# Two middle column blocks of an embedding gate joined into one, with three of eight pairs of k tiles in seven products

## The chip, the cores and the metric

The kernel runs on one core of a Trainium2 chip. The metric is device time in microseconds of one execution; a smaller number is better. PE is TensorE (the matmul engine), DVE is VectorE, ACT is ScalarE, SP is the engine that issues most DMAs. All matrices are float32. To get float32 accuracy from the fast matmul format, each operand is split into a high part (`hi`, a cast on ACT) and a low part (`lo`, the difference, a subtraction on DVE), and each product of two 128-row tiles takes three matmuls: low times high, high times high, high times low.

## The reference, cut to what matters

The layer is a decoder layer for 256 tokens of width 2048: a half feed-forward network (FFN), two token mixers, a second half FFN, each followed by a layer norm, and at the end a gated embedding:

```
ple = sigmoid(h @ w_ple_gate) * (p @ w_ple_proj)
h = layer_norm(alpha * h + ple, ln_g[3], ln_b[3])
```

`h` is 256 x 2048 (the result of the norm behind the second FFN), `w_ple_gate` is 2048 x 2048. The change touches only `h @ w_ple_gate`, a product with 16 k tiles of 128, two token halves of 128 and four column blocks of 512.

## The kernel before, in words

**Weights.** A weight chunk is two k tiles by 512 columns, 512 KB. `Chunk` loads it by one SP DMA into a 128x1024 tile (L105); `split` makes it into hi (ACT, L91) and lo (DVE, L92). All such tiles come from one pool of 46 (`SLOTS`).

**The planner.** `plan` is a list of units in the order of use. `Single` is one chunk: 1 tile loaded, 2 made, 12 units of "time". `Seven` is two chunks of the same pair of k tiles in neighbouring column blocks: 2 tiles loaded, 7 kept, time 21. `done(u)` after each unit frees its tiles and calls `fill`, which makes the next loaded unit as long as the time of the ready ones is under `ahead` (45 in this stage) and loads more while ready and loaded are under `far` (90), if the tiles allowed by `slots_for_weights` (24 here) suffice. Every engine runs its instructions in the order in which the Python code issues them, so `fill` also sets the order on DVE and ACT.

**Seven products.** `block` (L321) walks a list of units over a block of 1024 columns. For kind "P" it takes two chunks and adds for each its two k tiles for both token halves: 8 products. For kind "S" it treats two k tiles, two token halves and two column blocks as a 2x2 by 2x2 product and takes 7 products (a Strassen form). That needs four sums of weight tiles (`Seven.make`, L163 to L166, then splits), four sums of activation tiles (`seven_forms`, L362 to L366, then a split), four more PSUM banks, and a fold at the end of the last "S" unit (`seven_common`, L372 to L376). Both FFNs use it, for most blocks in the order "PPSPSPSP" or "PPSSPSSP".

**Side work.** `later(n, job)` puts a job into the list `side`; `run_side`, called after each chunk or unit, takes the first out and issues it.

**The embedding stage.** `embedding` (L1249) takes the four column blocks of the gate one after the other.
- Block 0 begins within the norm behind the second FFN (`norm.first`): six chunks for the first token half, then for the second, while DVE, PE and ACT norm, transpose and split the second half of `ht`, the activations. Then two chunks more.
- Blocks 1 and 2 take eight chunks each (`tokens_chunk`: 2 k tiles by 2 token halves by 3 matmuls = 12 matmuls a chunk).
- Each block has an epilogue per token half, `finish`: a sigmoid from PSUM (ACT, L1254), times the embedding projection, scaled sum with the residual and norm statistics (DVE, L1255 to L1257). The first half's epilogue is issued at the block's end, the second half's goes to `later(1)`, so it comes after the second chunk of the next block.
- Block 3 goes through `held_out` (L399): all eight chunks for the first token half, 6 matmuls each, then `first_done`, which issues that half's last epilogue and final layer norm (L478, L479), and then the eight chunks for the second half. Then the last epilogue, the second half's norm and the output follow with PE idle.

Of the kernel before, what the change touches and what calls it, by code (L numbers as in the profile page):

```python
# [8 lines left out]
F32 = mybir.dt.float32  # L9
F32R = mybir.dt.float32r  # L10
I32 = mybir.dt.int32
AF = mybir.ActivationFunctionType
ALU = mybir.AluOpType
PSUM = bass.MemoryType.PSUM

P = 128
S = 256
# [8 lines left out]
KD = D // P  # L26
# [10 lines left out]
SEVEN = (0, 1, 2, 3)  # L37
# [11 lines left out]
def layer(ctx: ExitStack, tc: tile.TileContext, io):  # L49
    nc = tc.nc  # L50
    sync, act, dve, pool, pe = nc.sync, nc.scalar, nc.vector, nc.gpsimd, nc.tensor
# [8 lines left out]
    def bank(name):  # L60
        return psum.tile([P, 512], F32, tag="ps", name=name)

    def banks(name):
        return [bank(name + str(j)) for j in range(2)]

    def slot(shape, dt, name):
        return slots.tile(shape, dt, tag="slot", name=name)
# [22 lines left out]
    def split(dst_hi, dst_lo, src, lo_engine=None):  # L90
        act.copy(dst_hi, src)  # L91
        (lo_engine or dve).tensor_tensor(dst_lo, src, dst_hi, ALU.subtract)  # L92
# [113 lines left out]
    def take(key):  # L206
        if not ready:
            fill(True)
        u = ready.pop(0)
        assert u.key == key, (u.key, key)  # L210
        return u

    def done(u):
        room["used"] -= u.keeps
        fill()
# [11 lines left out]
    def run_side(n=1):  # L227
        for _ in range(n):
            if side:
                side.pop(0)()  # L230
        if lazy and next(lazy[0], "end") == "end":
            lazy.pop(0)
# [62 lines left out]
    def half_of(a, t):  # L295
        return tuple(x[:, t * P : (t + 1) * P] for x in a)

    def tokens_chunk(chunk, k0, lhs, sums, ts, kks=(0, 1)):
        for t in ts:
            for kk in kks:  # L300
                sums[t].add(half_of(lhs(k0 + kk), t), chunk.columns(kk))
# [11 lines left out]
    def block_units(units, keys):  # L313

        for kind, p in units:
            if kind == "P":
                plan.extend(Single(keys(n, p)) for n in range(2))
            else:
                plan.append(Seven(keys(0, p), keys(1, p)))
# [35 lines left out]
    def seven_forms(full, hi, lo):  # L355


        a11, a21 = (full[:, 0::2, t * P : (t + 1) * P] for t in range(2))
        a12, a22 = (full[:, 1::2, t * P : (t + 1) * P] for t in range(2))
        raw = slot([P, 8, P], F32, "sums")  # L360
        f5, f6, f7, f3 = (raw[:, 2 * j : 2 * j + 2, :] for j in range(4))
        dve.tensor_tensor(f5, a21, a22, ALU.subtract)  # L362
        dve.tensor_tensor(f7, a11, a21, ALU.subtract)
        dve.tensor_tensor(f6, f5, a11, ALU.subtract)
        dve.tensor_tensor(f3, a12, f6, ALU.add)
        split(hi, lo, raw)  # L366
        return lambda e: [(hi[:, 2 * j + e, :], lo[:, 2 * j + e, :]) for j in range(4)]

    def seven_common(p1, p6, p7, q5):

        e, w = slot([P, 2, 512], F32, "eve"), slot([P, 2, 512], F32, "evw")
        act.copy(e[:, 0], p1)  # L372
        dve.tensor_tensor(w[:, 0], e[:, 0], p6, ALU.add)
        dve.tensor_tensor(e[:, 1], w[:, 0], p7, ALU.add)
        dve.tensor_tensor(w[:, 0], q5, w[:, 0], ALU.subtract)
        dve.tensor_tensor(w[:, 1], q5, e[:, 1], ALU.subtract)  # L376
        return e, w
# [6 lines left out]
    def plan_tokens(key, n_k, nk=2):  # L384
        for c in range(n_k // nk):
            plan.append(Single(key + (c,)))
# [69 lines left out]
    def ln_vectors(i):  # L456
        out = []
        for name in ("ln_g", "ln_b"):
            for hf in range(2):
                v = slot([P, 1024], F32, f"{name}{i}_{hf}")  # L460
                sync.dma_start(
                    v, io[name][0, i : i + 1, hf * 1024 : (hf + 1) * 1024].broadcast_to([P, 1024])
                )
                out.append(v)
        return out[:2], out[2:]
# [120 lines left out]
    def load_columns(src, col, name):  # L586
        v = slot([P, 2, 512], F32, f"{name}{col}")
        sync.dma_start(v, src[col])
        return v
# [48 lines left out]
    ht = big.tile([P, KD, 512], F32R, tag="ht", name="xt")  # L638
# [50 lines left out]
    def gu_units(j):  # L689
        if j == 0:  # L690
            return [("P", p) for p in range(KD // 2)]
        order = "PPSSPSSP" if j % 2 == 0 else "PPSPSPSP"
        sevens = list(SEVEN[: order.count("S")])
        plain = [p for p in range(KD // 2) if p not in sevens]
        return [(kind, (sevens if kind == "S" else plain).pop(0)) for kind in order]

    def gu_keys(name, j):
        return lambda n, p: (name + "_gu", j, n, p)
# [217 lines left out]
    def later(n, job):  # L916
        for j in range(n):
            if len(side) <= j:
                side.append(idle)
        side.insert(n, job)  # L920
# [325 lines left out]
        return norm  # L1246


    def embedding(ht, norm, y):  # L1249
        stats = small.tile([P, 2, 4, 6], F32, tag="stats", name="plst", bufs=1)  # L1250

        def finish(blk, ps, sg, t):
            sl = y[blk][:, t]
            act.activation(sg[:, t], ps, AF.Sigmoid)  # L1254
            dve.tensor_tensor(sg[:, t], sg[:, t], pp[blk][:, t], ALU.mult)  # L1255
            dve.scalar_tensor_tensor(sl, sl, ALPHA, sg[:, t], ALU.mult, ALU.add)
            dve.bn_stats(stats[:, t, blk, :], sl)  # L1257

        def last_norm(t, mv, rstd):
            rows = io["out"][0, t * P : (t + 1) * P]  # L1260
            for c in range(4):
                ln_normal(y, t, mv, rstd, g, b, 4 * c, 4)
                at = slice(c * 512, c * 512 + 512)
                (act if t and c % 2 else sync).dma_start(rows[:, at], y[c][:, t])

        lhs = lambda k: (ht[:, k, :S], ht[:, k, S:])
        for blk in range(4):
            pgs = banks(f"pg{blk}")
            sums = [Sum(b, KD) for b in pgs]
            sg = slot([P, 2, 512], F32, f"sg{blk}")  # L1270
            key = ("w_pg", blk)
            if blk == 0:
                for j in range(4):
                    pp[j] = load_columns(pp, j, "ppr")
                steps = [(key + (c,), 2 * c, 0) for c in range(FRONT)]
                norm.first(steps, lhs, [[s] for s in sums], (1, 3, 3, 6, 7, 9, 10))
                slots_for_weights(24)
                for c in range(FRONT, KD // 2):
                    u = take(key + (c,))
                    tokens_chunk(u.chunk, 2 * c, lhs, sums, (0, 1))  # L1280
                    done(u)
            elif blk < 3:
                for c in range(KD // 2):
                    u = take(key + (c,))
                    tokens_chunk(u.chunk, 2 * c, lhs, sums, (0, 1))
                    done(u)
                    run_side()
            if blk < 3:
                finish(blk, pgs[0], sg, 0)
                later(1, lambda blk=blk, pgs=pgs, sg=sg: finish(blk, pgs[1], sg, 1))  # L1290
                if blk == 0:
                    g, b = ln_vectors(3)
                continue

            def first_done():
                finish(3, pgs[0], sg, 0)
                last_norm(0, *ln_stats(stats[:, 0], 3, 0, LN_EPS))

            steps = [(key + (c,), 2 * c, 0) for c in range(KD // 2)]
            held_out(steps, lhs, [[s] for s in sums], lambda t, j: None, first_done, lambda n: None, False)  # L1300
            finish(3, pgs[1], sg, 1)
            last_norm(1, *ln_stats(stats[:, 1], 3, 1, LN_EPS))
# [30 lines left out]
    with tc.manual_schedule():  # L1333
        warm = small.tile([P, 1], F32, tag="nc1", name="warm")
        dve.memset(warm, 0.0)
        act.activation(warm, warm, AF.Silu)
        plan_ffn("f1")
        plan.extend(Single(("w_pp", blk, 0)) for blk in range(2))
        plan_mixers()
        plan.extend(Single(("w_pp", blk, 0)) for blk in range(2, 4))  # L1340
        plan_ffn("f2")
        for blk in range(4):
            plan_tokens(("w_pg", blk), KD)
        kept = sorted({p // 2 for p in SEVEN})
        norm = ffn("f1", 0, ht, None, x_parts, x_columns, (), rows[0])
        norm = mixers(norm.new, norm, rows[0], kept, rows[1])
        norm = ffn("f2", 2, norm.new, norm, norm.keep, rows[1], (), None)
        embedding(norm.new, norm, norm.y)
        assert not (plan or loaded or ready or side or lazy) and not room["used"]
# [100 lines left out]
```

## Time and profile before

| | us |
|---|---|
| median of 3 runs (lowest, highest) | 2313.45 (2310.71, 2315.56) |
| the profiled execution, its own time | 2312.8 |
| its span in the trace | 2311.0 |
| PE busy in the span | 2279.6 (99%) |
| DVE busy | 1871.4 (81%) |
| ACT busy | 1162.9 (50%) |

The span is the time between the first and the last instruction of the trace; the execution's own time is 1.8 us longer. A matmul row of 128x512 lasts 389 ns, but consecutive rows overlap, so that busy time is a count of time covered and not of durations added. Times in the trace are microseconds from the span's start. In a row of the timeline the columns are the start, the duration, the engine, the source line, the operation, and output and inputs with their shapes; a bracket at the end says how long the engine had been idle and what it waited for. A group of rows may be merged into one, with its count at the end.

The stage that is changed lies in the last 5% of the span: block 1 starts at 2231.0, block 2 at 2252.7, block 3 at 2274.4, and the last matmul ends at 2296.3.

### The profile page before, as it was taken

The page shows a single profiled execution, that of the slowest core. Times are in us where ns is not written, and L with a number is a line of the kernel's source. Part 1 is how long each engine was busy: PE and PEld are TensorE (multiplying, and loading weights), DVE is VectorE, ACT ScalarE, POOL GpSimd, SP SyncE. Part 2 cuts the span into 40 slices and gives each one's busy share as a digit, 9 for nine tenths or more (in the row PEclk, how much of TensorE's full clock was granted, in tenths as well). Part 3 has the DMA queues.
Part 4 walks back from the last instruction along what each step waited for, and adds up shares of the span by engine and source line. Part 5 has one row for each costly group of instructions (what it writes and reads, how often), then busy time and mean ns, then how long its engine had stood idle before and what let it go on. Part 6 is the DMA issues. An engine that isn't in the chain of part 4 may idle for free.

```text
span 2311.0 us, 28634 instructions
## 1 busy us (share of the span) xinstructions
PE 2279.6 (99%) x10502; PEld 1887.7 (82%) x10502; DVE 1871.4 (81%) x2348; ACT 1162.9 (50%) x1404; POOL 97.0 (4%) x53
## 2 busy tenths in 40 slices
PE   9999999999999999999999999999999999999997
PEld 7788888888887888888778888888888888888876
DVE  7999999988988874677655555779999999889876
ACT  5555555565553342434554543355565555655432
POOL 0000000000000530133000000000000000000000
PEclk9999999999999999999999999999999999999999
DMA  9566666665587565546556667476666566565771
GB/s 316 164 218 191 194 208 194 197 218 182 201 287 263 176 225 160 170 150 198 159 158 183 184 207 260 161 249 207 192 191 212 182 204 217 172 219 193 289 255 55
DMA packets 193725, 465.70 MB, mean 202 GB/s; under 512 B 14768, under 2 KB 16048, under 8 KB 193584
## 3 DMA queue, kind: packets, MB, share of 16 engines
q1 hardware_dynamic: 191456, 460.91, 60.7%
q10 hardware_dynamic: 2128, 2.97, 0.4%
q8 instruction: 82, 1.34, 0.2%
q14 instruction: 59, 0.48, 0.1%
HBM read 455.43 MB, written 8.39 MB: 201 GB/s over the span
## 4 chain that ended last, share of the span: by engine, by line
PE 95%; DVE 3%; issue 1%; DMA 0%; ACT 0%; DVEq 0%; ACTq 0%
PE f2g L293 3%; PE f2g L291 3%; PE f2g L292 3%; PE f1g L291 3%; PE gt L291 3%; PE f1g L292 3%; PE f1g L293 3%; PE rqk L242 3%; PE gt L292 3%; PE gt L293 3%; PE f2u L291 2%; PE f2u L292 2%; PE f2u L293 2%; PE f1u L292 2%; PE f1u L291 2%; PE f1u L293 2%
## 5 line engine op out<-in xcount | busy, mean ns | idle before, releaser
L92 DVE TENSOR_TENSOR lf_gu<-rf_gu,hf_gu 128x1024 fp32r<-128x1024 f32 (+1 forms) x283 | 334.5, 1215 | 10.1 <-ACT hf_gu L91 9.7
L91 ACT CAST hf_gu<-rf_gu 128x1024 fp32r<-128x1024 f32 (+1 forms) x283 | 282.0, 1046 | 19.1 <-DMA rf_gu<-in_f_gu 18.8
L92 DVE TENSOR_TENSOR lw_in_f<-rw_in_f,hw_in_f 128x1024 fp32r<-128x1024 f32 x148 | 208.2, 1439 | 61.7 <-ACT hw_in_f L91 59.1
L92 DVE TENSOR_TENSOR lf_down<-rf_down,hf_down 128x1024 fp32r<-128x1024 f32 x152 | 180.9, 1221 | 28.2 <-ACT hf_down L91 23.2
L91 ACT CAST hf_down<-rf_down 128x1024 fp32r<-128x1024 f32 x152 | 155.5, 1051 | 77.7 <-DMA rf_down<-in_f_down 24.4
L91 ACT CAST huf_gu<-uf_gu 128x1024 fp32r<-128x1024 f32 x70 | 73.8, 1054 | 158.9 <-DVE uf_gu L164 153.2
L91 ACT CAST hw_in_f<-rw_in_f 128x1024 fp32r<-128x1024 f32 x148 | 145.8, 1051 | 0.2
L291 PE MATMUL f1g<-hf_gu,xt 128*128 128x512 f32 x247 | 97.3, 394 | 5.3 <-ACT hf_gu L91 5.3
L291 PE MATMUL gt<-hw_in_f,ht 128*128 128x512 f32 x256 | 102.5, 400 | 0.0
L292 PE MATMUL gt<-hw_in_f,ht 128*128 128x512 f32 x256 | 99.9, 390 | 0.0
L293 PE MATMUL gt<-lw_in_f,ht 128*128 128x512 f32 x256 | 99.9, 390 | 0.0
L292 PE MATMUL f1g<-hf_gu,xt 128*128 128x512 f32 x247 | 96.9, 392 | 0.0
L293 PE MATMUL f1g<-lf_gu,xt 128*128 128x512 f32 x247 | 96.8, 392 | 0.0
L291 PE MATMUL f2g<-hf_gu,ht 128*128 128x512 f32 x247 | 96.5, 391 | 0.0
L293 PE MATMUL f2g<-lf_gu,ht 128*128 128x512 f32 x247 | 96.2, 389 | 0.0
L292 PE MATMUL f2g<-hf_gu,ht 128*128 128x512 f32 x247 | 96.1, 389 | 0.0
L91 ACT CAST hvf_gu<-vf_gu 128x1024 fp32r<-128x1024 f32 x70 | 73.8, 1055 | 29.7 <-DVE vf_gu L166 29.7
L92 DVE TENSOR_TENSOR luf_gu<-uf_gu,huf_gu 128x1024 fp32r<-128x1024 f32 x70 | 85.3, 1219 | 0.0
L92 DVE TENSOR_TENSOR lvf_gu<-vf_gu,hvf_gu 128x1024 fp32r<-128x1024 f32 x70 | 85.3, 1218 | 0.0
L795 ACT ACTIVATE eve<-eve 128x1024 f32<-128x1024 f32 x20 | 21.2, 1062 | 127.0 <-DVE eve L794 127.0
L291 PE MATMUL f2u<-hf_gu,ht 128*128 128x512 f32 x212 | 83.5, 394 | 0.0
L291 PE MATMUL f1u<-hf_gu,xt 128*128 128x512 f32 x212 | 83.3, 393 | 0.0
(1053 smaller groups left out, 6275.1 us busy)
## 6 DMA issues: line engine op xcount, KB each, us to landing
rf_gu<-in_f_gu SPq DMA_DIRECT2D x351, 512.0 KB, 5.0
rf_down<-in_f_down SPq DMA_DIRECT2D x176, 512.0 KB, 4.5
rw_in_f<-in_w_in_f SPq DMA_DIRECT2D x148, 512.0 KB, 4.1
rw_rv<-in_w_rv SPq DMA_DIRECT2D x32, 512.0 KB, 4.4
rw_ret<-in_w_ret SPq DMA_DIRECT2D x32, 512.0 KB, 4.2
rw_mix<-in_w_mix SPq DMA_DIRECT2D x32, 512.0 KB, 4.5
rw_pg<-in_w_pg SPq DMA_DIRECT2D x32, 512.0 KB, 4.8
rw_att<-in_w_att SPq DMA_DIRECT2D x16, 512.0 KB, 4.1
```

The source lines that it names most:

```text
L91: act.copy(dst_hi, src)
L92: (lo_engine or dve).tensor_tensor(dst_lo, src, dst_hi, ALU.subtract)
L242: pe.matmul(ps[f], hi[:, kk, f * P : (f + 1) * P], rhs(k), start=k == 0, stop=k == n_k - 1,)
L291: pe.matmul(o, al, bh, start=first, stop=False)
L292: pe.matmul(o, ah, bh, start=False, stop=False)
L293: pe.matmul(o, ah, bl, start=False, stop=self.left == 0)
L795: act.activation(g, g, AF.Silu)
```

## The change

Blocks 1 and 2 become one block of 1024 columns, run by `block` with the units `P3 P4 S0 P5 S1 P6 S2 P7` (the number is the pair of k tiles). The plan holds ten single chunks and three seven units for it, where there were sixteen chunks. Ahead of it, `forms_of` makes the activation sums of two groups of four k tiles: `whole` adds the high and low halves of `ht` back to full activations (the FFN had those at hand), then `seven_forms` follows. After the block four adds join the fold's result with the plain sums, and the four epilogues of blocks 1 and 2 go to `later(0)` to `later(3)`, that is, behind the first four chunks of block 3. Block 0 and block 3 keep their code; block 0's second epilogue is run by the joined block's second `run_side`. The order helper `units_of` is taken out of `gu_units` without a change to the FFNs.

```diff
+    def whole(parts, name):
+        full = slot([P, 4, S], F32, name)
+        n = 4 // len(parts)
+        for j, v in enumerate(parts):
+            dve.tensor_tensor(full[:, n * j : n * j + n], v[:, :, :S], v[:, :, S:], ALU.add)
+        return full
+
+    def forms_of(parts, name):
+        hi, lo = (slot([P, 8, P], F32R, name + w) for w in "hl")
+        return seven_forms(whole(parts, name + "w"), hi, lo)
+
+    def units_of(order, sevens):
+        sevens = list(sevens)
+        plain = [p for p in range(KD // 2) if p not in sevens]
+        return [(kind, (sevens if kind == "S" else plain).pop(0)) for kind in order]
+
+    def block_sums(ps, units, n_k):
+        s = sum(kind == "S" for kind, p in units)
+        return [[Sum(ps[t][n], n_k - (2 * s if t and n else s)) for n in range(2)] for t in range(2)]
...
+    PG_UNITS = units_of("PPSPSPSP", (0, 1, 2))
+    pg_keys = lambda n, p: ("w_pg", 1 + n, p)
...
-        for blk in range(4):
+        made = {}
+        for blk in (0, 1, 3):
+            key = ("w_pg", blk)
+            if blk == 1:
+                made.update((g, forms_of([ht[:, 4 * g : 4 * g + 4, :]], f"pgf{g}")) for g in range(2))
+                pgs = [banks(f"pg1{t}") for t in range(2)]
+                got = []
+                block(
+                    "pg", PG_UNITS, pg_keys, lhs, lambda p: made[p // 2](p % 2), block_sums(pgs, PG_UNITS, KD),
+                    lambda *a: got.extend(seven_common(*a)),
+                )
+                for n in range(2):
+                    for t in range(2):
+                        dve.tensor_tensor(got[n][:, t], got[n][:, t], pgs[t][n], ALU.add)
+                for j in range(4):
+                    n, t = j // 2, j % 2
+                    later(j, lambda n=n, t=t: finish(1 + n, got[n][:, t], got[n], t))
+                continue
...
-            elif blk < 3:
-                for c in range(KD // 2):
-                    u = take(key + (c,))
-                    tokens_chunk(u.chunk, 2 * c, lhs, sums, (0, 1))
-                    done(u)
-                    run_side()
-            if blk < 3:
-                finish(blk, pgs[0], sg, 0)
-                later(1, lambda blk=blk, pgs=pgs, sg=sg: finish(blk, pgs[1], sg, 1))
...
+                finish(0, pgs[0], sg, 0)
+                later(1, lambda pgs=pgs, sg=sg: finish(0, pgs[1], sg, 1))
...
-        for blk in range(4):
-            plan_tokens(("w_pg", blk), KD)
+        plan_tokens(("w_pg", 0), KD)
+        block_units(PG_UNITS, pg_keys)
+        plan_tokens(("w_pg", 3), KD)
```

## The prediction, on record before the changed kernel ran

> **What bounds the kernel now.** I read first the page's busy shares and chain, then the stretches of the embedding stage, then VectorE's order of work in it. The chain says that TensorE (PE) sets the time almost everywhere:
>
> ```profile
> PE 95%; DVE 3%; issue 1%; DMA 0%; ACT 0%; DVEq 0%; ACTq 0%
> ```
>
> The stretches show the changed place. The columns are the stretch, its length, then busy time of PE, weight load, VectorE (DVE), ScalarE (ACT), GpSimd, granted clock, DMA share, GB/s. Block 1 runs from 2231.0, block 2 from 2252.7, block 3 from 2274.4 (first token half) and 2285.3 (second); after 2296.3 comes the tail.
>
> ```profile
> 2226.00:2231.00 5.00, 5.00 (x24) 4.14 (x23) 5.00 (x5) 4.97 (x6) 0.00 (x0) 1.00 0.87 272
> 2231.00:2252.70 21.70, 21.70 (x97) 18.00 (x96) 13.96 (x16) 9.33 (x12) 0.00 (x0) 1.00 0.62 221
> 2252.70:2274.40 21.70, 21.70 (x97) 17.96 (x96) 13.07 (x15) 8.60 (x11) 0.00 (x0) 1.00 0.19 56
> 2274.40:2285.30 10.90, 10.90 (x50) 9.03 (x49) 8.15 (x10) 3.80 (x5) 0.00 (x0) 1.00 0.00 1
> 2285.30:2296.30 11.00, 11.00 (x50) 8.86 (x48) 9.49 (x20) 0.60 (x1) 0.00 (x0) 1.00 0.18 70
> ```
>
> PE has no gap from 2231.0 to 2296.3. VectorE is idle 7.7 us in block 1, 8.6 in block 2, 2.8 in block 3's first half: 19.1 us of cover until 2285.3. But in the 5 us before block 1 it has none: it comes out of the norm with its work in arrears, and its timeline shows that it reaches block 0's first epilogue only at 2231.35, when block 1 already runs:
>
> ```profile
> 2224.53 6.90 DVE L92 TENSOR_TENSOR lw_pg<-rw_pg,hw_pg 128x1024 fp32r<-128x1024 f32 x6 [0.26 <-ACT hw_pg L91]
> 2231.35 0.68 DVE L1255 TENSOR_TENSOR sg<-sg,ppr 128x512 f32<-128x512 f32 x1
> 2232.07 0.69 DVE L1256 SCALAR_TENSOR_TENSOR f2y<-f2y,sg 128x512 f32<-128x512 f32 x1
> 2232.79 0.69 DVE L1257 BATCH_NORM_STATS2 plst<-f2y 128x6 f32<-128x512 f32 x1
> ```
>
> **What is removed.** A plain pair of k tiles over two column blocks is 8 products of 3 matmuls, a seven-product pair is 7. Three such pairs save 9 matmuls. A row lasts 389 ns, but rows overlap; start to start is 21.70/96 = 0.226 us. So PE work falls from 192 to 183 matmuls, by **2.04 us** (0.09%). That is all the change can win here.
>
> **What is added, on VectorE.** Prices are start to start, since VectorE rows overlap slightly too. The nearest rows are those of the second half-FFN, which does the same (forms, then a seven unit):
>
> ```profile
> 1528.75 0.42 DVE L362 TENSOR_TENSOR sums<-keep 128x256 f32<-128x256 f32 x1
> ...
> 1531.75 1.23 DVE L92 TENSOR_TENSOR f2fl<-sums,f2fh 128x1024 fp32r<-128x1024 f32 x1 [1.45 <-ACT f2fh L91]
> 1532.89 0.42 DVE L362 TENSOR_TENSOR sums<-keep 128x256 f32<-128x256 f32 x1
> ...
> 1942.41 0.68 DVE L163 TENSOR_TENSOR uf_gu<-rf_gu,rf_gu 128x512 f32<-128x512 f32 x1
> ...
> 1945.14 1.22 DVE L92 TENSOR_TENSOR lf_gu<-rf_gu,hf_gu 128x1024 fp32r<-128x1024 f32 x1
> ...
> 1949.14 1.22 DVE L92 TENSOR_TENSOR f2al<-f2a,f2ah 128x1024 fp32r<-128x1024 f32 x1
> ```
>
> - Forms of one group: 1532.89 − 1528.75 = 4.14 us, the second there 3.82; both hold the wait for ACT's cast (1.45, 1.12), in which VectorE can do nothing else, as its order is fixed. Before each stands a new add of the halves of ht (128x1024, by `whole`). Before has no such add of two fp32r operands. Bounds: 0.61 us (half a 128x1024 row, if it ran at double rate) and 1.44 (the slowest such rows, L92 of w_in_f). I take 1.14, the step of the back-to-back L92 rows (6.90 us for 6), which has the same size and an fp32r operand. Two groups: 4.14 + 3.82 + 2.28 = **10.2 us**.
> - A seven unit's making: 1949.14 − 1942.41 = **6.73** us, against 4 x 1.14 = 4.56 for the four plain chunks it replaces.
> - The fold (L373 to L376) 2.71 us and four adds from PSUM (L794 rows) 2.41.
> - Epilogues (L1255 to L1257): 2.07 us each, as many as before, but the four of blocks 1 and 2 now all fall into block 3's first half instead of one.
>
> The planner's accounts decide the order. At block 1's start four plain chunks are ready (48 units of work, above the 45 it keeps ahead), as now. In VectorE's order: block 0's first epilogue, both forms, the first seven unit (made when the first chunk is done), block 0's second epilogue, two chunks, the second unit, two chunks, and so on. PE uses 24 matmuls (5.44 us) for a pair of plain chunks, 21 (4.76) for a seven unit.
>
> **The sum, step by step.** VectorE: epilogue 2231.35 to 2233.4; forms to 2243.7; first seven unit to 2250.4, its first low part (2.73 us in, 1.22 long) ready at 2247.6. PE: plain pairs 2231.0 to 2241.9, then the first seven unit, whose third matmul needs that low part: **a gap of about 5.3 us** (two matmuls inside it), until 2247.7, and the unit's end at 2252.0 instead of 2246.6. Its successor waits as well: VectorE does the epilogue to 2252.5 and the next chunk to 2253.7. From there VectorE keeps just ahead: units done at 2261.5 and 2270.5, PE's plain last pair ends at about 2279.5 (before: 2274.5). VectorE: two chunks of block 3 to 2275.0, fold to 2277.7, two more chunks to 2280.0, four adds to 2282.4. Then, in turn, one chunk (1.14) and one epilogue (2.07), four times. PE takes a chunk's first half in 6 matmuls, 1.36 us. Chunks 0 to 4 are in time; the low parts of chunks 5, 6, 7 are ready at 2286.8, 2290.0 and 2293.2, and PE waits 0.1, 1.8 and 1.9 us: **3.8 us**. The first half ends at 2294.2, the second (48 matmuls, 10.9) at 2305.1. Beside it VectorE has the last epilogue and the norm of the first token half, 10.0 us as now (2286.2 to 2296.2), so from 2295.2 to 2305.2: just hidden. The tail behind PE's end stays 14.7 us. PE's end was 2296.3, so the shift is 2305.1 − 2296.3 = **+8.8 us**; the 2.04 saved is in it.
>
> **The clock.** One cost more: after gaps PE is slowed. The trace has it before block 1:
>
> ```profile
> 2211.40:2215.00 3.60, 1.66 (x8) 1.08 (x9) 3.53 (x8) 0.74 (x2) 0.00 (x0) 0.99 0.02 5
> 2215.00:2218.40 3.40, 3.40 (x12) 2.72 (x11) 1.28 (x3) 0.59 (x1) 0.00 (x0) 0.50 0.78 230
> ```
>
> PE was busy 46% of 3.6 us, in pieces, and then had half clock for 3.4 us, worth 1.7. The 5.3 us gap will do the same, but the 1.7 lies in PE's slack, since VectorE is what PE waits for until block 3. In block 3 PE is busy 1.36 of each 3.2 us (42%) for two chunks; a half clock there lands on the second half, on the path. Bounds 0 and 1.7; I take 1.0, as the busy share is like the row's and part of the slow stretch would fall into the gaps. The Trainium skill, "TensorE: Matmul & The Clock Gate", section "What's actually happening", says that the clock falls back after an idle window of some 3.4 us. By it block 3, with no gap over 1.9 us, would keep its clock and the sum would stay +8.8; this case's trace speaks for more, since the longest gap before its drop was 2.0 us.
>
> Forecast: 2312.8 (the profiled execution; span 2311.0 and 1.8 around it) + 8.8 + 1.0 = **2322.6 us**. The median of before, 2313.45, is 0.65 higher, inside the spread of its runs (2310.71 to 2315.56), so I leave it.
>
> **Rivals.**
> 1. *TensorE stays the bound* (the other side). If the low parts come in time, only the saved 2.04 remains: 2310.8 us, no measurable change (below 0.2%, 4.6 us, this kernel's measurement can't tell). For it: 19.1 us of idle VectorE before, and an FFN that runs the same pattern of units with PE full. Against: the idle time lies late in each block, the debt at its start. It decides at 2241.9: the first unit's low part must be there, so the 16.3 us from 2231.35 to 2247.6 would have to be 10.6. Chance 0.08.
> 2. *Only the first gap counts.* If block 3's epilogues fit beside its chunks, PE's lateness at 2279.5 remains: +4.8, 2317.6. For it: VectorE would only need some 4 us less in 62. Against: the four epilogues are 8.3 us in a stretch of 10.9 that has to hold five makings too. Chance 0.14.
> 3. *Tiles run out.* Forms (4 tiles), three units (7 each while in use) and block 3's tiles share 46. A raw load or a making that must wait until PE releases a tile closes the circle: PE waits for VectorE, VectorE for PE. In this stage SP already waits for PE before loads, 6.8 us at longest. One such wait on the path: 2322.6 + 6.8 = 2329.4. Against: loads are issued some 90 units, 20 us of PE time, ahead. Chance 0.14.
> 4. *Faster by over 0.2%*: would need more than the saved matmuls give. Chance 0.03. That the product count isn't cut is excluded by the unit list.
>
> **How the numbers follow.** The forecast, 2319 to 2327, gets 0.61. The range takes in rivals 2 and most of 3 and leaves out 1 and 4: 2316 to 2329.5. Slower by over 0.2% (above 2318.1): 0.61 + 0.14 + about half of 0.14 = 0.83; within: 0.08 + the other half = 0.14; faster 0.03.
>
> **What would show it.** In the profile after: 183 PE matmuls in the joined block; a PE gap of about 5 us near 2242 that names VectorE's low part of the first unit; forms from 2233 to 2244 on VectorE; gaps of near 2 us before chunks 6 and 7 of block 3; clock 0.50 behind the first gap, perhaps behind the last. The prediction is wrong if VectorE starts the forms earlier, if the first unit is made before them, or if the 128x1024 add of ht takes far less than 1.14 us.

## The result and the profile after

The changed kernel takes **2322.56 us** (median of 5 runs, 2322.02 to 2325.44) against 2313.45 (5 runs, 2310.71 to 2315.56); the ratio is 1.0043, 95% interval 1.0029 to 1.0058. The forecast was 2322.6 within 2316 to 2329.5. The profiled execution took 2322.76 us with a span of 2321.0, 10.0 us more than before.

The stretches of the embedding stage in the changed kernel (columns as in the prediction: length, busy time of PE, weight load, VectorE, ScalarE, GpSimd, clock, DMA share, GB/s):

```profile
2231.00:2252.00 21.00, 16.23 (x65) 12.67 (x64) 18.43 (x26) 10.37 (x13) 0.00 (x0) 0.88 0.39 119
2252.00:2279.00 27.00, 27.00 (x117) 22.27 (x116) 26.59 (x32) 15.26 (x18) 0.00 (x0) 0.97 0.64 220
2279.00:2295.00 16.00, 13.59 (x59) 10.64 (x58) 15.76 (x21) 5.04 (x7) 0.00 (x0) 1.00 0.00 1
2295.00:2306.00 11.00, 11.00 (x51) 9.04 (x49) 10.44 (x22) 0.60 (x1) 0.00 (x0) 1.00 0.16 61
```

PE, full throughout before, is now busy 16.23 of the first 21.00 us and 13.59 of 16.00 in the third stretch. VectorE, which had 7.7 and 8.6 us to spare in blocks 1 and 2, is busy 26.59 of 27.00. PE's timeline names what it waits for at both places. First the start of the first seven unit:

```profile
2242.93 0.39 PE L293 MATMUL pg<-lw_pg,ht 128*128 128x512 f32 x1
2244.65 0.50 PE L291 MATMUL pgs<-hw_pg,ht 128*128 128x512 f32 x1 [1.33 <-ACT hw_pg L91]
2244.99 0.39 PE L292 MATMUL pgs<-hw_pg,ht 128*128 128x512 f32 x1
2248.82 0.79 PE L293 MATMUL pgs<-lw_pg,ht 128*128 128x512 f32 x1 [3.44 <-DVE lw_pg L92]
```

then the last two chunks of block 3's first token half:

```profile
2289.82 0.39 PE L292 MATMUL pg<-hw_pg,ht 128*128 128x512 f32 x1
2291.09 0.50 PE L293 MATMUL pg<-lw_pg,ht 128*128 128x512 f32 x1 [0.89 <-DVE lw_pg L92]
...
2292.36 0.40 PE L292 MATMUL pg<-hw_pg,ht 128*128 128x512 f32 x1
2294.28 0.50 PE L293 MATMUL pg<-lw_pg,ht 128*128 128x512 f32 x1 [1.52 <-DVE lw_pg L92]
```

Each wait is for a low part, or (the first) for ScalarE's cast of the first unit's weights, queued behind the cast of the activation sums; from 2232 to 2307 PE waits for nothing else. And VectorE's timeline shows why the low part is late: the activation sums stand between block 0's first epilogue and the first seven unit.

```profile
2234.70 1.21 DVE L374 TENSOR_TENSOR pgf0w<-ht 128x1024 f32<-128x1024 f32 x1
...
2238.61 1.23 DVE L92 TENSOR_TENSOR pgf0l<-sums,pgf0h 128x1024 fp32r<-128x1024 f32 x1 [1.11 <-ACT pgf0h L91]
2239.76 1.22 DVE L374 TENSOR_TENSOR pgf1w<-ht 128x1024 f32<-128x1024 f32 x1
...
2243.68 1.23 DVE L92 TENSOR_TENSOR pgf1l<-sums,pgf1h 128x1024 fp32r<-128x1024 f32 x1 [1.11 <-ACT pgf1h L91]
2244.82 0.69 DVE L163 TENSOR_TENSOR uw_pg<-rw_pg,rw_pg 128x512 f32<-128x512 f32 x1
...
2247.55 1.22 DVE L92 TENSOR_TENSOR lw_pg<-rw_pg,hw_pg 128x1024 fp32r<-128x1024 f32 x1
```

The two brackets are all the waits that VectorE has on its way. From block 0's first epilogue (2232.65) to the start of block 3's last low part (2293.01) it is idle for 2.6 of 60.4 us, and 2.2 of them are these two waits for ScalarE's casts of the sums.

Totals of single executions carry a spread from earlier stages. In the eight kernels with the same code up to block 1 (before, changed, a1 to a6), block 0's first epilogue starts on VectorE anywhere from 2229.8 to 2234.6 us (before 2231.35, changed 2232.65). So the experiments are read by two lengths that leave this out. The **stage** runs from that epilogue's first VectorE row to the start of PE's last matmul, the **chain** from it to the first VectorE row of the last epilogue, behind which only the tail follows. Both are read from one profiled execution of each kernel. The ratios are to runs of before made beside that kernel (medians 2313.45 to 2314.44), so they differ a little from quotients of the medians in the table.

| kernel | median us | ratio to before, 95% interval | stage us | chain us |
|---|---|---|---|---|
| before | 2313.45 | | 64.68 | 65.73 |
| changed | 2322.56 | 1.0043 (1.0029 to 1.0058) | 73.34 | 74.39 |
| a1, joined, plain pairs only | 2313.94 | 0.9998 (0.9990 to 1.0007) | 64.68 | 65.73 |
| a2, seven units last | 2322.45 | 1.0038 (1.0025 to 1.0052) | 73.25 | 74.30 |
| a3, a third of the block's matmuls left out | 2320.96 | 1.0032 (1.0020 to 1.0045) | 73.38 | 74.44 |
| a4, two seven units | 2316.33 | 1.0008 (0.9999 to 1.0017) | 66.66 | 67.72 |
| a5, without the adds of ht | 2319.67 | 1.0028 (1.0018 to 1.0037) | 70.83 | 71.89 |
| a6, these adds twice | 2324.76 | 1.0049 (1.0035 to 1.0063) | 75.84 | 76.89 |
| b1, two units, early sums | 2313.13 | 0.9996 (0.9987 to 1.0005) | 63.34 | 64.40 |
| b2, three units, early sums, GpSimd | 2317.22 | 1.0013 (1.0005 to 1.0022) | 63.53 | 64.58 |
| b4, three units, early sums, VectorE | 2316.53 | 1.0010 (1.0001 to 1.0019) | 64.09 | 68.39 |

### The profile page after: what moved, and what is told of

The parts are those of the page before. It is cut to its first block, busy times and chain, and to the rows that moved or that the text cites. A ratio compares the mean times of both kernels' runs of the same rounds, so it can differ in the third digit from the quotient of the medians.

```text
span 2321.0 us, 28679 instructions
## 1 busy us (share of the span) xinstructions
PE 2282.4 (98%) x10493; PEld 1888.6 (81%) x10493; DVE 1897.1 (82%) x2386; ACT 1170.8 (50%) x1413; POOL 97.0 (4%) x53
## 3 DMA queue, kind: packets, MB, share of 16 engines
q8 instruction: 82, 1.34, 0.2%
## 4 chain that ended last, share of the span: by engine, by line
PE 93%; DVE 5%; issue 1%; ACT 0%; DMA 0%; DVEq 0%; ACTq 0%
PE f2g L293 3%; PE f2g L291 3%; PE f2g L292 3%; PE gt L291 3%; PE f1g L291 3%; PE f1g L293 3%; PE f1g L292 3%; PE rqk L242 3%; PE gt L292 3%; PE gt L293 3%; PE f2u L291 2%; PE f2u L292 2%; PE f2u L293 2%; PE f1u L291 2%; PE f1u L292 2%; PE f1u L293 2%
## 5 line engine op out<-in xcount | busy, mean ns | idle before, releaser
L92 DVE TENSOR_TENSOR lf_gu<-rf_gu,hf_gu 128x1024 fp32r<-128x1024 f32 (+1 forms) x283 | 334.4, 1215 | 9.7 <-ACT hf_gu L91 9.1
L92 DVE TENSOR_TENSOR lw_in_f<-rw_in_f,hw_in_f 128x1024 fp32r<-128x1024 f32 x148 | 208.2, 1439 | 61.7 <-ACT hw_in_f L91 59.4
L92 DVE TENSOR_TENSOR lf_down<-rf_down,hf_down 128x1024 fp32r<-128x1024 f32 x152 | 181.0, 1220 | 28.6 <-ACT hf_down L91 22.3
L92 DVE TENSOR_TENSOR luf_gu<-uf_gu,huf_gu 128x1024 fp32r<-128x1024 f32 x70 | 85.3, 1218 | 0.0
L92 DVE TENSOR_TENSOR lvf_gu<-vf_gu,hvf_gu 128x1024 fp32r<-128x1024 f32 x70 | 85.2, 1218 | 0.0
```

## The experiments

The theory: from block 0's first epilogue on, VectorE has no slack left, and its work up to block 3's last low part sets the time; PE's 2.04 us saved don't count. The rivals: the position of the first seven unit, the bunched epilogues, waits for tiles or PSUM banks, and PE's clock.

### a1: the joined block without seven products

```diff
-    PG_UNITS = units_of("PPSPSPSP", (0, 1, 2))
+    PG_UNITS = units_of("PPPPPPPP", ())
...
-                made.update((g, forms_of([ht[:, 4 * g : 4 * g + 4, :]], f"pgf{g}")) for g in range(2))
...
-                    later(j, lambda n=n, t=t: finish(1 + n, got[n][:, t], got[n], t))
+                    later(j, lambda n=n, t=t, ps=pgs[t][n]: finish(1 + n, ps, got[n], t))
```

> The two blocks joined, but with eight plain pairs: no activation sums, no seven units, no fold; the four epilogues still come in block 3's first half. Stage = from VectorE's first epilogue row of block 0 to the start of PE's last matmul: 64.7 us in the kernel before, 73.3 in the changed one. Theory (VectorE's debt: its added work from 2231 on is what sets the time): nothing is added, so stage 64.7 +- 0.5, time as before (2313 +- 2), no PE gap in the joined block or block 3. Rival (the four epilogues in block 3's first half cost by themselves the gaps before its last chunks): stage 67 to 68.5.

Measured: stage 64.68, to the hundredth that of before, and no PE gap over 0.7 us. Joining the blocks and bunching four epilogues costs nothing by itself: before the first of the four VectorE sits idle for 13.5 us with five of block 3's eight chunks made, and it makes the other three between the epilogues in time. The rival with the epilogues falls; they cost only what VectorE is already behind.

### a2: the same work, seven units last

```diff
-    PG_UNITS = units_of("PPSPSPSP", (0, 1, 2))
+    PG_UNITS = units_of("PPPPPSSS", (0, 1, 2))
```

> Same work in another order: five plain pairs first, the three seven units last. Theory (VectorE's total work until block 3's last chunk sets the time): the gap of 5 us before the first seven unit goes (2 to 3 us remain before the third plain pair), but block 3's low parts come no earlier: stage 73.3 +- 0.7, time as the changed kernel; the lost time moves into gaps before block 3's chunks 4 to 7. Rival (the first gap is a cost of its own, made by the position of the first seven unit): stage 68 to 69, time some 4.5 us under the changed kernel.

Measured: stage 73.25, against 73.34. The gap at the first seven unit is gone; two of 1.7 and 1.1 us remain before the third plain pair, and four of 1.9 to 2.0 us stand before block 3's chunks 4 to 7. PE's clock is 1.00 through the whole stage here, so the slow clock of the changed kernel was no cost of its own either, and neither was the first gap. The order of the units moves the waiting about and leaves its sum.

### a3: a third of the joined block's matmuls left out

```diff
-            pe.matmul(o, al, bh, start=first, stop=False)
-            pe.matmul(o, ah, bh, start=False, stop=False)
+            if not self.two:
+                pe.matmul(o, al, bh, start=first, stop=False)
+            pe.matmul(o, ah, bh, start=first and self.two, stop=False)
```

(`two` is set for the sums of the joined block.)

> In the joined block the low x high matmul of each product is left out (the output lacks that term): 61 of its 183 matmuls, 13.8 us of PE work. VectorE's and ScalarE's work is unchanged. Theory (VectorE sets the time): stage 73.3 +- 0.7, up to 1.7 more if a longer gap halves PE's clock on the path; time as the changed kernel. Rival (PE's own work still counts in the stage): stage 60 to 66, time 7 to 14 us under the changed kernel.

Measured: stage 73.38. Taking 13.8 us of PE work out of the stage gains nothing. This is the plainest sign that PE is no longer the bound there: all of the 13.8 us turned into gaps (steps of 5.3 and 4.2 us at the first seven unit, of 1.9 before each of block 3's chunks 5 to 7, and smaller ones between) and into slower matmuls behind the first of them (clock 0.50 from 2246 to 2252).

### a4: two seven units of one group

```diff
-    PG_UNITS = units_of("PPSPSPSP", (0, 1, 2))
+    PG_UNITS = units_of("PPSPPSPP", (0, 1))
-                made.update((g, ...) for g in range(2))
+                made.update((g, ...) for g in range(1))
```

> Two seven units of one group instead of three of two, in the order P P S P P S P P: one set of activation sums and one unit less on VectorE (5.1 + 2.2 us), PE saves 6 matmuls (1.36 us) instead of 9. Theory, by the same ledger: no gap over 0.3 us in the joined block, one gap of 1.0 to 1.7 us before block 3's last chunk; stage 64.5 to 65.5, time 2313 to 2315. Rival (each seven unit or each set of sums costs by waiting for tiles or PSUM banks, not by VectorE's time): a gap before the first unit stays at 3 us or more, stage 67 or more.

Measured: stage 66.66, 1.2 us above the range, and 2316.33 us where 2313 to 2315 was expected. The gap at the first seven unit is gone, which speaks against the rival; but a step of 1.39 us stands at the plain chunk behind it, which I had left out. Its low part comes after that unit's making and an epilogue, while PE needs it as soon as the unit's products are done. The second, a step of 1.84 us before block 3's last chunk, loses 1.6 us, as expected. The same ledger gives the first one once that row is in it, so I put the miss down to the reckoning and not to the theory.

### a5 and a6: the same two adds left out, and made twice

```diff
-        return seven_forms(whole(parts, name + "w"), hi, lo)
+        return seven_forms(parts[0][:, :, :S].bitcast(F32), hi, lo)
```
```diff
-            dve.tensor_tensor(full[:, n * j : n * j + n], v[:, :, :S], v[:, :, S:], ALU.add)
+            for _ in range(2):
+                dve.tensor_tensor(full[:, n * j : n * j + n], v[:, :, :S], v[:, :, S:], ALU.add)
```

> The two adds that put ht's halves together (1.25 us of VectorE each, start to start) are left out; the activation sums are made of the high halves alone (the output lacks the low part there). Theory (the stage lasts as long as VectorE's chain): 2.5 us less, stage 73.3 - 2.5 = 70.8 +- 0.4, all of it out of the gap before the first seven unit and the gaps of block 3 unchanged or shorter by the same sum. Rival (part of the loss is not VectorE's time: PE's slower clock behind the gap, tiles or banks): stage 72 or more.

> The same two adds made twice, 2.5 us more on VectorE. Theory: stage 73.3 + 2.5 = 75.8 +- 0.4. Rival (the chain has slack somewhere, so that the first part of a further delay is hidden): stage 75 or less.

Measured: 70.83 and 75.84, that is 2.51 less and 2.50 more for 2.5 us of VectorE's time. Microsecond for microsecond, in both directions: the stage is VectorE's chain (with the two waits for ScalarE's casts of the sums in it, 2.2 us in each of these kernels), without slack and without a part that belongs to tiles, banks or the clock. One detail of a5's expectation failed: the gaps of block 3 did not stay or shrink. Its first gap loses 2.7 us instead of 5.1, but block 3's two lose 3.4 instead of 2.7, because PE now comes to block 3 earlier against VectorE's last low parts.

### b1: two units, sums made in the norm's gaps

VectorE idles in the norm ahead of block 1 (before: 2.1, 1.6 and 1.1 us while it waits for ScalarE's casts). Group 0 of `ht` is final by then. `norm.first` gets a hook behind a given step:

```diff
+    def forms_parts(ht, g, eng):
...
-        def first(self, steps, lhs, sums, times):
+        def first(self, steps, lhs, sums, times, extra={}):
...
+                extra.get(j + 1, idle)()
...
-    PG_UNITS = units_of("PPSPSPSP", (0, 1, 2))
+    PG_UNITS = units_of("PPSPPSPP", (0, 1))
...
-                made.update((g, forms_of([ht[:, 4 * g : 4 * g + 4, :]], f"pgf{g}")) for g in range(2))
...
+                    lambda j: slots_for_weights(24, 96, 140) if j == 6 else None,
...
-                norm.first(steps, lhs, [[s] for s in sums], (1, 3, 3, 6, 7, 9, 10))
+                full, sums0, high, low, made[0] = forms_parts(ht, 0, dve)
+                norm.first(
+                    steps, lhs, [[s] for s in sums], (1, 3, 3, 6, 7, 9, 10),
+                    {6: full, 8: lambda: (sums0(), high()), 9: low},
+                )
```

`forms_parts` gives the making of one group's sums as four jobs (the add of the halves, the sums, the cast, the low part). The function with `j` is called ahead of unit `j` of the block; there it raises the planner's `ahead` to 96 and `far` to 140. So b1 differs from a4 in two things, which were not run apart.

> Two seven units of one group; its activation sums are made in VectorE's idle gaps within the norm, ahead of block 1; the planner may make all of block 3's chunks ahead of the fold. By the ledger VectorE then has 4 us to spare and PE is the bound: no gap over 0.5 us in the joined block or block 3, stage 64.7 - 1.36 = 63.3, up to 64.0; time 1.0 to 1.4 us under the kernel before, if nothing is lost in the norm. Rival (the early sums push the norm's own steps on VectorE back): block 0 ends later, and the time does not fall.

Measured: stage 63.34, what PE alone needs (64.68 less 1.36), without a gap over 0.7 us. The stretches from the joined block on, as in the first view above:

```profile
2232.00:2275.00 43.00, 43.00 (x191) 35.61 (x191) 40.70 (x47) 25.71 (x30) 0.00 (x0) 1.00 0.46 171
2275.00:2286.00 11.00, 11.00 (x50) 9.10 (x49) 8.77 (x14) 1.51 (x3) 0.00 (x0) 1.00 0.00 0
```

PE is full again, at full clock, beside a VectorE that is busy 40.70 of 43.00 us. Block 0 ends no later than in the other kernels (first epilogue at 2233.09, within their 2229.8 to 2234.6). The total, 0.9996 (0.9987 to 1.0005), can't be told from before: 1.36 us is 0.06%. It is the one version here in which the seven products pay in the stage and nothing is lost ahead of it or behind it.

### b2 and b4: three units, group 1's adds on GpSimd or on VectorE

b2 adds to b1's edits, with the units of the change:

```diff
+                full1, sums1, high1, low1, made[1] = forms_parts(ht, 1, pool)
...
-                    {6: full, 8: lambda: (sums0(), high()), 9: low},
+                    {6: full, 8: lambda: (sums0(), high(), full1(), sums1()), 9: low},
...
-                    lambda j: slots_for_weights(24, 96, 140) if j == 6 else None,
+                    lambda j: (high1(), low1()) if j == 3 else slots_for_weights(24, 96, 140) if j == 6 else None,
```

b4 has `dve` for `pool` there, and calls `full1` and `sums1` at j == 3 too, no longer within the norm.

> Three seven units; group 0's sums in VectorE's gaps within the norm, group 1's adds on GpSimd, its cast and low part before the second seven unit; block 3's chunks made ahead as in b1. VectorE's chain is 9.0 us shorter than in the changed kernel, so its end comes about 1 us behind PE's: stage 62.6 (PE alone) to 64.3; time 0.5 to 2 us under the kernel before. Rival (GpSimd's adds slow VectorE's rows beside them, or end too late for the second unit): L92 rows of 128x1024 of 1.4 us instead of 1.22 while GpSimd works, a gap before the third seven unit, stage 65 or more.

> As b2, but group 1's adds on VectorE, before the second seven unit, instead of on GpSimd within the norm. Theory (GpSimd's adds beside VectorE's made both slow and held the norm up in b2): no PE gap of 3.7 us near the third transposes of the norm, block 0's first epilogue back at about 2232 to 2233.5. VectorE's chain is 3.9 us longer than b2's behind that point: from its first epilogue of block 0 to the last epilogue 68.5 us (before 65.7, changed 74.4, b1 64.4, b2 64.6); PE's last matmul not later than 64.5, so that the surplus stands as VectorE's arrears behind PE's end. Time 2.5 to 3.5 us over the kernel before. Rival (the early sums of group 0 alone hold the norm up when three units follow): the gap in the norm stays.

b2: stage 63.53, as the theory has it, but the time is 1.0013 of before (1.0005 to 1.0022), slower where 0.5 to 2 us less was expected. The rival's signs (a gap before the third seven unit, a stage of 65) don't show, but its cause does, ahead of the stage: the first epilogue starts only at 2237.0, later than in any kernel with the old code up to block 1. GpSimd's adds in the norm, and VectorE's rows beside them:

```profile
2220.56 2.51 POOL L386 TENSOR_TENSOR pgf1w<-ht 128x1024 f32<-128x1024 f32 x1 [1149.88 <-DVE ht L92]
2223.14 0.80 POOL L394 TENSOR_TENSOR sums<-pgf1w 128x256 f32<-128x256 f32 x1
```

```profile
2220.40 0.41 DVE L394 TENSOR_TENSOR sums<-pgf0w 128x256 f32<-128x256 f32 x1
2220.73 2.62 DVE L395 TENSOR_TENSOR sums<-pgf0w 128x256 f32<-128x256 f32 x1
2223.27 0.96 DVE L396 TENSOR_TENSOR sums<-sums,pgf0w 128x256 f32<-128x256 f32 x1
2224.26 0.83 DVE L397 TENSOR_TENSOR sums<-pgf0w,sums 128x256 f32<-128x256 f32 x1
2225.01 1.21 DVE L531 SCALAR_TENSOR_TENSOR f2y<-f2y,mv,ln_g 128x512 f32<-128x512 f32 x1
```

A subtraction of 0.42 us took 2.62, about as long as GpSimd's add beside it, and a norm step of 0.74 took 1.21. PE waits for the norm step behind that one:

```profile
2227.50 1.09 PE L539 MATMUL lnps<-ident,f2y 128*128 128x128 f32 x4 [3.31 <-DVE f2y L532]
```

It started 3.7 us after the matmul ahead of it. In b4, where VectorE makes these adds, the gap in the norm is gone (first epilogue at 2232.64), and the chain is 68.39, as the ledger had it (68.5). PE's last matmul is early (stage 64.09), but VectorE starts the last epilogue 4.3 us behind it (1.05 before); the time, 1.0010 of before (1.0001 to 1.0019), is slower by 0.2 to 4.4 us where 2.5 to 3.5 was expected. Neither version with three units comes out ahead: in b2 the stage itself gets shorter, but the norm pays for it, and in b4 VectorE's work reaches beyond PE's. Two units fit.

## Why the prediction was right, point by point

- **What the change saves**, 2.04 us of PE work for 9 matmuls: right, and right that it doesn't count (a3: even 13.8 us doesn't). b1 shows that such a saving is real once VectorE keeps up: 1.34 us of stage for 6 matmuls, 1.36 expected.
- **VectorE's debt at the start**: right. The forms take 2234.70 to 2244.82, 10.1 us (predicted 10.2: the two adds of ht take 1.25 each from start to start instead of the 1.14 taken, the rest 3.8 for each group instead of 4.14 and 3.82). The prediction's upper bound for such a row, 1.44, was misread: it is the mean of the w_in_f rows, of which one lasts 2.31. The gap at the first unit: the two PE steps of 1.72 and 3.83 us, less 0.45 for two matmuls, are 5.1 us lost (predicted 5.3).
- **The second loss**, before block 3's last chunks: steps of 1.27 and 1.92 us, less 0.45, are 2.7 us (predicted 3.8). The stage as a whole grew by 73.34 − 64.68 = 8.66 us against the 8.8 of the sum. The gap is shorter because PE came 0.6 us later into block 3 than the sum had it; what counts, VectorE's last low part, starts 60.36 us behind the first epilogue (predicted 2292.0 − 2231.35 = 60.65).
- **Slack behind the first gap**: right that a slow clock there costs nothing, but not in the way the sum was filled. The sum's end of the joined block, 5.0 us later than before, holds about 1.7 us of waits behind the first gap (5.3 − 2.04 + 1.7). No such waits came. PE's clock was 0.50 for 4.3 us there instead (2249.4 to 2253.7), slower steps cost 2.6 us in the joined block, and block 3 began 5.6 us later, counted from VectorE's first epilogue. a2, which loses 2.4 us around that place instead of 5.1 and keeps clock 1.00, has the same stage. The whole of PE's account closes: −2.04 saved, +7.8 in the four gaps, +2.8 in slower steps, together the 8.66 but for 0.1.
- **The clock term, +1.0 us: wrong.** Block 3 kept clock 1.00. a2 puts it to a harder test, four such gaps in a row, here in its stretches:

```profile
2284.00:2288.00 4.00, 2.38 (x9) 1.66 (x10) 3.90 (x7) 2.20 (x4) 0.00 (x0) 1.00 0.00 0
2288.00:2292.00 4.00, 2.47 (x11) 1.48 (x9) 3.90 (x6) 0.00 (x0) 0.00 (x0) 1.00 0.00 0
2292.00:2296.00 4.00, 2.48 (x11) 1.96 (x11) 3.93 (x6) 0.60 (x1) 0.00 (x0) 1.00 0.01 2
```

  The step that failed is "the busy share is like the row's": I set a share of matmul steps (1.36 of 3.2 us, 42%) beside a share of busy rows (46%). By rows, a2's stretches are 60 to 62% busy. What the Trainium skill says in "TensorE: Matmul & The Clock Gate", section "What's actually happening", of a whole idle window of 3.4 us gives block 3 rightly (no gap over 1.9 us, clock 1.00). It doesn't by itself give the drop in the norm before block 1, where the longest gap was 2.0 us, nor the one in a5: there the clock was 0.50 from 2244.2 to 2247.2, behind a single gap of 2.92 us (2.54 idle) that followed full work. How long or how dense the idle time must be, these runs don't show.
- **Why the total fitted nevertheless.** The profiled executions differ by 10.0 us: 8.7 in the stage and 1.3 ahead of it (2232.65 − 2231.35), where the eight kernels with this code are spread over 4.8 us. The forecast's 1.0 for the clock stood where that 1.3 stands. By the medians the difference is 9.1. The 8.8 is borne out; the agreement of the totals to 0.1 us is chance.
- **The rivals.** TensorE as the bound: refuted by a3, and made true by b1, where the debt is gone. Only the first gap: refuted by the changed kernel itself, which loses 2.7 us before block 3's last chunks; a2 adds that the first gap is no cost of its own. Running out of tiles: no wait for a tile or a bank shows among PE's or VectorE's, and a5 and a6 leave no part of the loss for it. What was not tried is to fill the 2.2 us in which VectorE waits for ScalarE's casts of the sums.

## What to carry to other kernels

An engine that is 81% busy on average can still have no slack at the stage that is changed: find the point where it comes out of the stage before with arrears, and add up its work from there to the last result that the bounding engine needs. When a change trades matmuls for vector work, the trade counts only as far as that chain has room, and reordering units didn't make room here; moving work to where the engine truly idles did. A dose test, one suspected operation left out and once doubled, tells in two runs whether a chain has slack.

## What the runs showed of the hardware that I had not expected

GpSimd and VectorE held each other up: beside GpSimd's add of 128x1024 (2.51 us), a VectorE subtraction of 128x256 took 2.62 us instead of 0.42, and the following rows 0.96 and 0.83 instead of 0.42, all with two operands from SBUF. The Trainium skill, "SBUF — State Buffer", section "Who interferes with whom", says that a VectorE instruction with two SBUF inputs contends with a GpSimd instruction that reads SBUF, because they share a read interface; these rows agree. The trace of before already had such rows, in the mixers: a row of L92 (128x1024) at 784.46 took 2.31 us instead of 1.22 beside GpSimd's row of L892 (783.53 to 785.69). GpSimd's own L891 rows (128x512) took 2.28 us at 781.18, beside L92 rows all the while, and 1.28 at 1018.48, with an L92 row beside only the last 0.45 us. In b2, 6.2 us of GpSimd work (2220.56 to 2226.80) cost about 4 us of VectorE's time: that is more than the 2.8 us which the moved adds take on VectorE itself.
